# One hybrid decoder block on one core: the x, q and k projections of groups 1 to 7 take 512-column matmuls, one output half after the other

## The chip, the core and the metric

The kernel runs on one core of a Trainium2 chip. A core has a matrix engine (TensorE, PE in the profile, with its weight loads as PEld), a vector engine (VectorE, DVE), a scalar engine (ScalarE, ACT), GpSimd (POOL) and SyncE (SP), which issues most of the DMAs. Each engine works through its own list of instructions in the order in which the program was built and waits on semaphores for the others. The metric is device time in microseconds (us) for one execution; less is better.

## What is computed

The reference is one layer of a hybrid block on 256 tokens of 1024 channels, all in float32:

```python
hn = rmsnorm(x, norm1_w)
proj = hn @ w_in
z, xbc_raw, dt_raw, q, k, v, g_raw = jnp.split(proj, IN_OFFSETS, axis=-1)
...
y_ssd = ssd_mixer(z, xbc_raw, dt_raw, ...)       # x, B, C through a causal conv of 4 taps and SiLU, then the scan
q = partial_rope(q.reshape(b, s, ATT_N_HEADS, ATT_HEAD_DIM), pos)
k = partial_rope(k.reshape(b, s, ATT_N_HEADS, ATT_HEAD_DIM), pos)
y_att = moba_attention(q, k, v.reshape(b, s, ATT_N_HEADS, ATT_HEAD_DIM))
gates = jax.nn.sigmoid((g_raw + b_gate).astype(jnp.float32)).astype(x.dtype)
merged = g_ssd * (y_ssd @ w_ssd_proj) + g_att * (y_att @ w_att_proj)
x = x + merged @ w_out
h2 = rmsnorm(x, norm2_w)
a, gb = jnp.split(h2 @ w_ffn_up, 2, axis=-1)
a = causal_dwconv(a, ffn_conv_w, ffn_conv_b)
x = x + (jax.nn.silu(a) * gb) @ w_ffn_down
```

A final rmsnorm follows. The change is in `hn @ w_in`, in the columns that become x (the scan's input), q and k.

## The kernel before

**Products in two parts.** A float32 product is made of products of rounded parts. Each weight tile `raw` (128 partitions, 8 k-tiles of 256 columns, 1 MB) is split into a high part `hi` (an ACT copy that rounds, L95) and a rest `lo = raw - hi` (DVE, L103), each in two halves of 4 k-tiles. The activations `hn` are pairs in the same way: `hn[k][:, 0]` high, `hn[k][:, 1]` low, 256 tokens each, side by side. `mm_unit` (L145) makes, for each k-tile and each of two output halves m of 128 columns, three matmuls of 256 columns into the same sums: high weight by high (L164), high by low (L165), low weight by high (L166). That is 48 matmuls in a unit.

**Units and groups.** The weights come in units of 1 MB. Each of the 8 groups g has six units: bc (B and C), x, qk, then z and two of the gates for even g, or v and z for odd g (group 1 has no v; in group 7 z stands ahead of v). `next_unit` splits one unit ahead. `hi` and `lo` have 4 buffers of half a unit each, so a half of unit n+2 can be split when the same half of unit n has been read for the last time. The order of TensorE is the order in which the code is written; the order on ACT and DVE is made by a scheduler when the program is built, by priority and its own estimates of time.

**What stands between the units.** PSUM tiles `mm` have 3 buffers, taken in turn: one for each unit, two for a pair of gate units. After the unit bc, `conv_silu` (L382) reads its sums out of PSUM: an ACT pass makes `cacc`, three DVE steps (L391) add the other taps, for each of two halves, then `th` (ACT, L394) and the product (DVE, L395). x goes the same way. The unit qk is copied out by ACT to `qkraw` (L433), from which POOL's DMAs take the swapped rows for the rotation and DVE makes `qk` (L439). `small_1(g)` stands between the units x and qk on TensorE: the scan's products `py` of the group before (L519), the scores `s_ps` (L548), the attention output `po` (L585) and the broadcast `pb` (L241). On DVE and ACT the same step brings `yg` (L523, L524, L535), the softmax (L555 to L563), and the pairs `yatt` and `yn` (L203, L204).

Further on, the up projection's `mm_wide` (L168) makes the high weight's two products in one matmul of 512 columns (L174), then the low weight's in one of 256 (L178); its two sums meet when they are read out (L865, L866).

Of the kernel before, what the change touches and what calls it, by code (L numbers as in the profile page):

```python
# [8 lines left out]
F32 = mybir.dt.float32  # L9
F32R = mybir.dt.float32r  # L10
I32 = mybir.dt.int32
AF = mybir.ActivationFunctionType
ALU = mybir.AluOpType
PSUM = bass.MemoryType.PSUM
DRAM = bass.MemoryType.DRAM
PE_ONLY = {mybir.EngineType.PE}
IN_ORDER = {mybir.EngineType.PE, mybir.EngineType.Activation, mybir.EngineType.DVE}

P = 128
T = 256  # L20
# [21 lines left out]
def block_kernel(tc, xtok_d, head_d, par_d, nf_d, con_d, rope_d, win_d, wgate_d, bg_d, watt_d, wssd_d, wout_d, wup_d, wdn_d, out_d):  # L42
    nc = tc.nc
    st = ExitStack()
    pool = lambda name, bufs=1, **kw: st.enter_context(tc.tile_pool(name=name, bufs=bufs, **kw))
    with st:
# [36 lines left out]
        def new_pair(name):  # L83
            return pairs.tile([P, 2, T], F32R, tag="pair", bufs=32, name=name)
# [8 lines left out]
        def split_high(raw, k0, n):  # L93
            hi = wpool.tile([P, 4, 256], F32R, tag="hi", bufs=4, name="hi")
            split_half.hi = nc.scalar.activation(hi[:, :n], raw[:, k0 : k0 + n], AF.Copy)  # L95
            return hi
# [36 lines left out]
        def next_unit():  # L133

            i = next_unit.i
            next_unit.i += 1
            load_to(i + 3)
            while len(units) < min(i + 2, len(seq)):
                n = len(units)
                units.append(split_unit(raws[n], seq[n][1]))  # L140
            return units[i]
# [3 lines left out]
        def mm_unit(ps, halves, act, first=True, last=True, k0=0, apart=False):  # L145


            tiles = [(hi, lo, kk) for hi, lo, n in halves for kk in range(n)]
            nk = len(tiles)
            km = [(k, m) for k in range(nk) for m in range(2)]  # L150
            if apart:
                km.sort(key=lambda x: x[1])
                ps = [p[:, 0, :] for p in ps]
            else:
                ps = [ps[:, m, :] for m in range(2)]
            with tc.manual_schedule(engines=PE_ONLY):
                for k, m in km:
                    hi, lo, kk = tiles[k]
                    xh, xl = act[k0 + k][:, 0, :], act[k0 + k][:, 1, :]
                    wh = hi[:, kk, m * P : m * P + P]  # L160
                    wl = lo[:, kk, m * P : m * P + P]
                    a = first and k == 0 and (m == 0 or apart)
                    z = last and k == nk - 1 and (m == 1 or apart)
                    nc.tensor.matmul(ps[m], wh, xh, start=a, stop=False)  # L164
                    nc.tensor.matmul(ps[m], wh, xl, start=False, stop=False)  # L165
                    nc.tensor.matmul(ps[m], wl, xh, start=False, stop=z)  # L166
# [31 lines left out]

        def mm_tile():
            return ps_mm.tile([P, 2, T], F32, tag="mm", bufs=3, name="mm")  # L200

        def split_pair(dst, src):
            nc.scalar.activation(dst[:, 0, :], src, AF.Copy)  # L203
            nc.vector.tensor_tensor(dst[:, 1, :], src, dst[:, 0, :].bitcast(F32), op=ALU.subtract)  # L204
# [70 lines left out]
        flat = lambda ap: ap.rearrange("p a b -> p (a b)")  # L275
# [5 lines left out]
        hn = [new_pair("hn") for _ in range(KD)]  # L281
# [3 lines left out]
        with tc.manual_schedule(engines=IN_ORDER):  # L285
# [64 lines left out]
            for k in range(4):  # L350
                normed(k)
                for m in range(2):
                    nc.tensor.matmul(psbc[:, m], raws[0][:, k, m * P : m * P + P], hnf[k], start=(k == 0 and m == 0),
                                     stop=False)
# [3 lines left out]
            hi = split_high(raws[0], 4, 4)  # L358
# [38 lines left out]
        S = [dict() for _ in range(NG)]  # L397
# [11 lines left out]

        def u_x(g):  # L410
            hv = next_unit()
            ps = mm_tile()
            mm_unit(ps, hv, hn)
            xs = S[g]["xs"] = ssp.tile([P, 2, T], F32, tag="xs", bufs=2, name="xs")
            if g:
                conv_silu(xs, ps, (2 * g, 2 * g + 1))
            else:
                S[g]["x_ps"] = ps
# [5 lines left out]
        def u_qk(g):  # L424
            hv = next_unit()
            if g == 0:

                with tc.issue_after(split_half.lo.ins):
                    conv_silu(S[0]["xs"], S[0]["x_ps"], (0, 1))
            ps = mm_tile()  # L430
            mm_unit(ps, hv, hn)
            raw = atp.tile([P, 2, T], F32, tag="qkraw", bufs=1, name="qkraw")
            S[g]["qk_copy"] = nc.scalar.activation(raw, ps, AF.Copy)  # L433
            sw = swaps[g % 2]
            nc.gpsimd.dma_start(sw[48:80:2], raw[49:80:2])
            nc.gpsimd.dma_start(sw[49:80:2], raw[48:80:2])
            qk = S[g]["qk"] = atp.tile([P, 2, T], F32, tag="qk", bufs=2, name="qk")
            cosb = rope[:, 0:1, :].to_broadcast([P, 2, T])
            nc.vector.tensor_tensor(qk, raw, cosb, op=ALU.mult)  # L439
# [206 lines left out]
        atp = st_at.enter_context(tc.tile_pool(name="atp", bufs=1))  # L646
# [143 lines left out]
        for h in range(2):  # L790
            ps = [mm_tile(), mm_tile()]
# [4 lines left out]
            for c in range(2):  # L796
                m = half(mt[:, c], h)
# [33 lines left out]
        hv = next_unit()  # L831
# [7 lines left out]
        act = []  # L839
        first = []  # L840
        for f in range(2):
            hv, ps = next_unit(), mm_tile()
# [7 lines left out]
        for f in range(NF):  # L850
            ab = work.tile([P, 2, T], F32, tag="ab", bufs=2, name="ab")
            if f < 2:
                hv, ps = first[f]
# [5 lines left out]
            else:  # L859
# [3 lines left out]
                hv, ps = next_unit(), up.tile([P, 2, 2, T], F32, tag="up", bufs=2, name="up")  # L863
# [60 lines left out]
        for h in range(2):  # L924
            ps = [mm_tile(), mm_tile()]
            for k0, _ in DOWN[:-1]:
                mm_tok(ps, next_unit(), act, k0, NF)
            hv, k0 = next_unit(), DOWN[-1][0]
# [129 lines left out]
```

## Time and profile before

| | |
|---|---|
| median of 3 runs | 597.99 us (595.78 to 967.97) |
| profiled execution | 595.27 us, its span 593.5 us, so 1.77 us lie around the span |
| granted clock of TensorE | 0.998 |
| busy | PE 584.9 us (99%), DVE 458.8 us (77%), ACT 375.6 us (63%) |
| groups 1 to 7 | x units from about 60 us to 282 us into the span |

Matmuls overlap in their pipeline, so the time that a matmul takes from the engine is the distance from its start to the next one's start, not the duration shown beside it. The same holds on DVE and ACT to a lesser degree.

### The profile page before, as it was taken

What the parts mean: (1) busy time and instruction counts of PE and PEld (TensorE: products, weight loads), DVE (VectorE), ACT (ScalarE), POOL (GpSimd) and SP (SyncE); (2) the same over time, 40 slices, a digit from 0 to 9 for tenths busy, and PEclk for the clock granted to TensorE, in tenths of its full rate; (3) what the DMA queues carried; (4) which work ended last, traced back from release to release, by engine and by line L of the source; (5) the groups of instructions that cost most, each with busy time, mean ns of one, the idle gap of its engine ahead of it and who ended that gap; (6) DMA issues with size and microseconds to landing.
All of it is one profiled execution on the core that took longest, in us unless ns stands there. A gap on an engine that the chain in (4) does not pass through costs nothing.

```text
span 593.5 us, 9945 instructions
## 1 busy us (share of the span) xinstructions
PE 584.9 (99%) x3832; PEld 525.8 (89%) x3832; DVE 458.8 (77%) x891; ACT 375.6 (63%) x673; POOL 21.2 (4%) x41
## 2 busy tenths in 40 slices
PE   9999999999999999999999999999999999999994
PEld 8998999999999999999988888889888888888884
DVE  3896989888897888978896546667888898884643
ACT  2855696957769577695786333456877777774432
POOL 0010010100001000010000000000000000000100
PEclk9999999999999999999999999999999999999999
DMA  8666626662646526565345765545456456464611
GB/s 307 259 193 242 236 105 233 207 213 89 217 174 206 202 97 213 180 192 204 109 145 168 293 195 172 200 163 193 151 204 214 170 184 214 139 219 149 233 43 71
DMA packets 17936, 109.74 MB, mean 185 GB/s; under 512 B 2256, under 2 KB 2512, under 8 KB 6240
## 3 DMA queue, kind: packets, MB, share of 16 engines
q1 hardware_dynamic: 15120, 100.42, 48.2%
q0 software_dynamic: 2336, 6.85, 4.2%
q10 hardware_dynamic: 432, 1.84, 0.8%
q8 instruction: 30, 0.49, 0.3%
q14 instruction: 18, 0.15, 0.1%
HBM read 107.49 MB, written 1.08 MB: 183 GB/s over the span
## 4 chain that ended last, share of the span: by engine, by line
PE 99%; DVE 0%; issue 0%; ACT 0%; DVEq 0%; ACTq 0%
PE up L174 12%; PE mm L164 11%; PE mm L165 11%; PE mm L166 11%; PE mm L195 11%; PE mm L196 11%; PE mm L197 11%; PE up L178 6%; PE py L519 2%; PE mm L293 1%; PE s_ps L548 1%; PE po L585 1%; PE mm L458 1%; PE mm L459 1%; PE mm L460 1%; PE pt_ps L571 1%
## 5 line engine op out<-in xcount | busy, mean ns | idle before, releaser
L103 DVE TENSOR_TENSOR lo<-raw,hi 128x1024 fp32r<-128x1024 f32 x183 | 222.9, 1223 | 72.9 <-ACT hi L95 71.1
L95 ACT ACTIVATE hi<-raw 128x1024 fp32r<-128x1024 f32 x183 | 191.8, 1056 | 126.7 <-PE mm L197 64.1
L164 PE MATMUL mm<-hn,hi 128*128 128x256 f32 x504 | 143.6, 285 | 0.0
L165 PE MATMUL mm<-hn,hi 128*128 128x256 f32 x504 | 142.6, 283 | 0.0
L166 PE MATMUL mm<-hn,lo 128*128 128x256 f32 x504 | 142.5, 283 | 0.0
L164 PEld LDWEIGHTS mm<-hn,hi 128*128 128x128 f32 x504 | 96.7, 192 | 0.5 <-ACT hi L95 0.3
L165 PEld LDWEIGHTS mm<-hn,hi 128*128 128x128 f32 x504 | 96.7, 192 | 0.2
L166 PEld LDWEIGHTS mm<-hn,lo 128*128 128x128 f32 x504 | 96.7, 192 | 0.0
L174 PE MATMUL up<-xw,hi 128*128 128x512 f32 x320 | 76.3, 391 | 0.0
L174 PEld LDWEIGHTS up<-xw,hi 128*128 128x128 f32 x320 | 58.8, 188 | 11.4
L391 DVE SCALAR_TENSOR_TENSOR cacc<-mm,par,cacc 128x255 f32<-128x255 f32 (+2 forms) x96 | 44.4, 475 | 0.7
L178 PEld LDWEIGHTS up<-xw,lo 128*128 128x128 f32 x320 | 41.0, 191 | 1.6
L178 PE MATMUL up<-xw,lo 128*128 128x256 f32 x320 | 41.5, 283 | 0.0
L196 PE MATMUL mm<-lo,act 128*128 128x512 f32 (+1 forms) x92 | 35.0, 380 | 0.0
L195 PE MATMUL mm<-hi,act 128*128 128x512 f32 (+1 forms) x92 | 34.9, 380 | 0.0
L197 PE MATMUL mm<-hi,act 128*128 128x512 f32 (+1 forms) x92 | 34.9, 380 | 0.0
L875 DVE SCALAR_TENSOR_TENSOR facc<-ab,par,facc 128x255 f32<-128x255 f32 (+1 forms) x44 | 21.2, 483 | 11.4 <-ACT facc L873 10.6
L195 PE MATMUL mm<-hi,hn 128*128 128x512 f32 x64 | 25.4, 397 | 0.0
L195 PE MATMUL mm<-hi,yn 128*128 128x512 f32 x64 | 25.2, 394 | 0.0
L197 PE MATMUL mm<-hi,hn 128*128 128x512 f32 x64 | 25.0, 390 | 0.0
L196 PE MATMUL mm<-lo,hn 128*128 128x512 f32 x64 | 25.0, 390 | 0.0
L197 PE MATMUL mm<-hi,yn 128*128 128x512 f32 x64 | 24.9, 390 | 0.0
(208 smaller groups left out, 970.8 us busy)
## 6 DMA issues: line engine op xcount, KB each, us to landing
raw<-in_win_dram SPq DMA_DIRECT2D x34, 1024.0 KB, 4.8
raw<-in_wup_dram SPq DMA_DIRECT2D x22, 1024.0 KB, 4.8
raw<-in_wdn_dram SPq DMA_DIRECT2D x10, 1024.0 KB, 4.8
raw<-in_wgate_dram SPq DMA_DIRECT2D x8, 1024.0 KB, 5.3
raw<-in_wssd_dram SPq DMA_DIRECT2D x8, 1024.0 KB, 4.9
acsB<-acsT_d POOLq DMA_DIRECT2D x8, 512.0 KB, 5.8
raw<-in_watt_dram SPq DMA_DIRECT2D x4, 1024.0 KB, 5.3
raw<-in_wout_dram SPq DMA_DIRECT2D x4, 1024.0 KB, 5.2
```

Of the source, the lines that this page charges most:

```text
L95: split_half.hi = nc.scalar.activation(hi[:, :n], raw[:, k0 : k0 + n], AF.Copy)
L103: split_half.lo = nc.vector.tensor_tensor(lo[:, :n], raw[:, k0 : k0 + n], hi[:, :n].bitcast(F32), op=ALU.subtract)
L164: nc.tensor.matmul(ps[m], wh, xh, start=a, stop=False)
L165: nc.tensor.matmul(ps[m], wh, xl, start=False, stop=False)
L166: nc.tensor.matmul(ps[m], wl, xh, start=False, stop=z)
L174: nc.tensor.matmul(ps[:, m].rearrange("p a b -> p (a b)"), hi[:, kk, m * P : m * P + P], act[k].rearrange("p a b -> p (a b)"), start=(k == ...
L178: nc.tensor.matmul(ps[:, m, 1], lo[:, kk, m * P : m * P + P], act[k][:, 0, :], start=False, stop=(k == len(tiles) - 1))
L195: nc.tensor.matmul(o, xh, wh, start=(k == 0 if apart else k0 + k == 0), stop=False)
L196: nc.tensor.matmul(o, xh, wl, start=False, stop=False)
L197: nc.tensor.matmul(o, xl, wh, start=False, stop=(k0 + k == nk - 1))
L391: nc.vector.scalar_tensor_tensor(acc[:, s:], src[:, m, : T - s], w(m, 3 - s), acc[:, s:], op0=ALU.mult, op1=ALU.add)
L875: nc.vector.scalar_tensor_tensor(acc[:, s:], src[:, : T - s], w(2 - s), acc[:, s:], op0=ALU.mult, op1=ALU.add)
```

## The change

For g of 1 to 7, `u_x` and `u_qk` call `mm_sum` in place of `mm_unit`. It makes output half m = 0 in full, then m = 1, each in a PSUM tile of its own: 8 matmuls of 512 columns (high weight, both parts of hn), then 8 of 256 columns (low weight, high part of hn) that add to the second part of the tile. Each half is read out on its own: ACT copies the second part to SBUF, DVE adds the first part. For x the sum lands in a new tile `xsum`, from which `conv_silu` now reads; it has the tag and the single buffer of `qkraw`. Group 0, bc, z, v and the gates stay as they are.

```diff
+        def mm_sum(dst, halves, act):
+
+
+            tiles = [(hi, lo, kk) for hi, lo, n in halves for kk in range(n)]
+            for m in range(2):
+                ps = mm_tile()
+                with tc.manual_schedule(engines=PE_ONLY):
+                    for k, (hi, lo, kk) in enumerate(tiles):
+                        nc.tensor.matmul(flat(ps), hi[:, kk, m * P : m * P + P], flat(act[k]), start=(k == 0), stop=False)
+                    for k, (hi, lo, kk) in enumerate(tiles):
+                        nc.tensor.matmul(ps[:, 1], lo[:, kk, m * P : m * P + P], act[k][:, 0, :], start=False,
+                                         stop=(k == len(tiles) - 1))
+                mm_sum.copy = nc.scalar.activation(dst[:, m], ps[:, 1], AF.Copy)
+                nc.vector.tensor_tensor(dst[:, m], ps[:, 0], dst[:, m], op=ALU.add)
...
         def u_x(g):
             hv = next_unit()
-            ps = mm_tile()
-            mm_unit(ps, hv, hn)
+            if g:
+                ps = atp.tile([P, 2, T], F32, tag="qkraw", bufs=1, name="xsum")
+                mm_sum(ps, hv, hn)
+            else:
+                ps = mm_tile()
+                mm_unit(ps, hv, hn)
...
-            ps = mm_tile()
-            mm_unit(ps, hv, hn)
-            raw = atp.tile([P, 2, T], F32, tag="qkraw", bufs=1, name="qkraw")
-            S[g]["qk_copy"] = nc.scalar.activation(raw, ps, AF.Copy)
+            if g:
+                raw = atp.tile([P, 2, T], F32, tag="qkraw", bufs=1, name="qkraw")
+                mm_sum(raw, hv, hn)
+                S[g]["qk_copy"] = mm_sum.copy
+            else:
+                ps = mm_tile()
+                mm_unit(ps, hv, hn)
+                raw = atp.tile([P, 2, T], F32, tag="qkraw", bufs=1, name="qkraw")
+                nc.scalar.activation(raw, ps, AF.Copy)
```

The scheduler makes another order of it. In the changed kernel a line's number is larger by 15 (from L214 on) or 24 (behind `u_qk`); the sum on DVE is L215 and the copy on ACT is L214.

DVE, group 1, before, from the first step of bc's conv on. `mm_674` is the PSUM tile of bc, `raw_758` the weight of z1, the unit behind qk1:

```order
L391 SCALAR_TENSOR_TENSOR cacc_727<-mm_674,par_75,cacc_727 128x255
L391 SCALAR_TENSOR_TENSOR cacc_727<-mm_674,par_75,cacc_727 128x254
L391 SCALAR_TENSOR_TENSOR cacc_727<-mm_674,par_75,cacc_727 128x253
L391 SCALAR_TENSOR_TENSOR cacc_728<-mm_674,par_75,cacc_728 128x255
L103 TENSOR_TENSOR lo_887<-raw_758,hi_885 128x1024
L395 SCALAR_TENSOR_TENSOR bc_726<-th_734,cacc_727 128x256
L391 SCALAR_TENSOR_TENSOR cacc_728<-mm_674,par_75,cacc_728 128x254
L391 SCALAR_TENSOR_TENSOR cacc_728<-mm_674,par_75,cacc_728 128x253
L103 TENSOR_TENSOR lo_891<-raw_758,hi_889 128x1024
L395 SCALAR_TENSOR_TENSOR bc_726<-th_740,cacc_728 128x256
```

The same place in the changed kernel:

```order
L406 SCALAR_TENSOR_TENSOR cacc_727<-mm_674,par_75,cacc_727 128x255
L406 SCALAR_TENSOR_TENSOR cacc_727<-mm_674,par_75,cacc_727 128x254
L215 TENSOR_TENSOR xsum_768<-mm_769,xsum_768 128x256
L406 SCALAR_TENSOR_TENSOR cacc_727<-mm_674,par_75,cacc_727 128x253
L406 SCALAR_TENSOR_TENSOR cacc_728<-mm_674,par_75,cacc_728 128x255
L406 SCALAR_TENSOR_TENSOR cacc_814<-xsum_768,par_75,cacc_814 128x255
L410 SCALAR_TENSOR_TENSOR bc_726<-th_734,cacc_727 128x256
L406 SCALAR_TENSOR_TENSOR cacc_728<-mm_674,par_75,cacc_728 128x254
L406 SCALAR_TENSOR_TENSOR cacc_814<-xsum_768,par_75,cacc_814 128x254
L406 SCALAR_TENSOR_TENSOR cacc_728<-mm_674,par_75,cacc_728 128x253
L406 SCALAR_TENSOR_TENSOR cacc_814<-xsum_768,par_75,cacc_814 128x253
L215 TENSOR_TENSOR xsum_768<-mm_791,xsum_768 128x256
```

The two splits of z1 have left this place, and x's sums and conv steps stand among bc's.

DVE, group 1, before, some 20 instructions further on, at the end of the softmax's first passes; `raw_883` is the weight of bc of group 2:

```order
L555 ISA pr_871,sm_872<-s_ps_856,con_76 128x256
L555 ISA sm_872 128x1
L103 TENSOR_TENSOR lo_955<-raw_883,hi_953 128x1024
L557 TENSOR_SCALAR sm_872<-sm_872 128x2
L103 TENSOR_TENSOR lo_959<-raw_883,hi_957 128x1024
```

The same place in the changed kernel, where `raw_758` is z1's weight as above and `raw_876` bc's of group 2:

```order
L579 ISA pr_864,sm_865<-s_ps_849,con_76 128x256
L579 ISA sm_865 128x1
L103 TENSOR_TENSOR lo_880<-raw_758,hi_878 128x1024
L581 TENSOR_SCALAR sm_865<-sm_865 128x2
L103 TENSOR_TENSOR lo_884<-raw_758,hi_882 128x1024
L585 RECIPROCAL sm_855<-sm_855 128x2
L215 TENSOR_TENSOR qkraw_886<-mm_887,qkraw_886 128x256
L103 TENSOR_TENSOR lo_939<-raw_876,hi_937 128x1024
```

The splits of z1 stand here now, and those of bc behind them. In groups 3, 5 and 7 it is the same: both splits of the unit behind qk (v, v and z) move from between bc's conv steps to behind the second L535. In groups 2, 4 and 6 the first split of z stays among the conv steps and the second moves to behind the second L535.

ACT, group 1, before, from bc's conv on:

```order
L387 ACTIVATE cacc_727<-mm_674,par_75 128x256
L387 ACTIVATE cacc_728<-mm_674,par_75 128x256
L95 ACTIVATE hi_885<-raw_758 128x1024
L394 ACTIVATE th_734<-cacc_727 128x256
L95 ACTIVATE hi_889<-raw_758 128x1024
L387 ACTIVATE cacc_821<-mm_768,par_75 128x256
```

And in the changed kernel:

```order
L402 ACTIVATE cacc_727<-mm_674,par_75 128x256
L402 ACTIVATE cacc_728<-mm_674,par_75 128x256
L214 ACTIVATE xsum_768<-mm_769 128x256
L402 ACTIVATE cacc_814<-xsum_768,par_75 128x256
L409 ACTIVATE th_734<-cacc_727 128x256
L95 ACTIVATE hi_878<-raw_758 128x1024
L95 ACTIVATE hi_882<-raw_758 128x1024
L214 ACTIVATE xsum_768<-mm_791 128x256
```

Both high copies of z1 stand ahead of the copy of x's second half, and behind the first conv pass of x's first half, which waits for the sum on DVE.

## Rows read from the trace of the kernel before

**Rows 1.** The page: span, busy time by engine, and the chain's shares by engine.

```profile
span 593.5 us, 9945 instructions
PE 584.9 (99%) x3832; PEld 525.8 (89%) x3832; DVE 458.8 (77%) x891; ACT 375.6 (63%) x673; POOL 21.2 (4%) x41
...
PE 99%; DVE 0%; issue 0%; ACT 0%; DVEq 0%; ACTq 0%
```

**Rows 2.** Windows from small_1(2) to (3) to (4): PE, PEld, DVE, ACT, POOL busy, clock, DMA.

```profile
93.50:133.40 39.90, 39.90 (x297) 36.67 (x298) 34.97 (x74) 27.83 (x57) 2.61 (x5) 1.00 0.62 206
133.40:168.00 34.60, 34.60 (x296) 33.31 (x296) 30.23 (x67) 24.88 (x53) 1.54 (x3) 1.00 0.49 166
```

**Rows 3.** Waits of the weight loads: the one for a split, in total.

```profile
PEld mm L164 <- ACT hi L95: 0.3, 1, 0.3
```

**Rows 4.** Timeline of PE inside an `mm_unit`: start, duration, instruction.

```profile
149.79 0.28 PE L166 MATMUL mm<-hn,lo 128*128 128x256 f32 x1
...
150.15 0.28 PE L166 MATMUL mm<-hn,lo 128*128 128x256 f32 x1
```

**Rows 5.** The chain in the up projection: start, length, what.

```profile
414.61 3.65 PE up L174 x16
418.27 1.91 PE up L178 x16
420.18 3.65 PE up L174 x16
```

**Rows 6.** Groups of instructions by line and shape: busy us, mean ns, idle before.

```profile
L391 DVE SCALAR_TENSOR_TENSOR cacc<-mm,par,cacc 128x255 f32<-128x255 f32 x32 | 15.2, 476 | 0.0
...
L875 DVE SCALAR_TENSOR_TENSOR facc<-ab,par,facc 128x255 f32<-128x255 f32 x22 | 10.6, 483 | 10.6 <-ACT facc L873 10.6
...
L857 DVE TENSOR_TENSOR ab<-mm,rb 128x256 f32<-128x256 f32 x2 | 0.8, 417 | 0.0
...
L203 ACT ACTIVATE yatt<-po 128x256 fp32r<-128x256 f32 x8 | 3.0, 381 | 6.4 <-PE po L585 6.4
```

**Rows 7.** Timeline of DVE in group 1 (no idle between these rows).

```profile
65.10 1.90 DVE L391 SCALAR_TENSOR_TENSOR cacc<-mm,par,cacc 128x255 f32<-128x255 f32 x4
66.92 1.22 DVE L103 TENSOR_TENSOR lo<-raw,hi 128x1024 fp32r<-128x1024 f32 x1
68.05 0.42 DVE L395 SCALAR_TENSOR_TENSOR bc<-th,cacc 128x256 f32<-128x256 f32 x1
68.39 0.99 DVE L391 SCALAR_TENSOR_TENSOR cacc<-mm,par,cacc 128x254 f32<-128x254 f32 x2
...
76.67 1.22 DVE L103 TENSOR_TENSOR lo<-raw,hi 128x1024 fp32r<-128x1024 f32 x1
```

**Rows 8.** Timeline of PE in group 1: end of small_1, start of qk1.

```profile
67.22 0.93 PE L548 MATMUL s_ps<-qk 64*128 64x128 f32 x8
68.08 0.39 PE L164 MATMUL mm<-hn,hi 128*128 128x256 f32 x1
```

**Rows 9.** Timeline of DVE in group 3.

```profile
129.83 1.91 DVE L391 SCALAR_TENSOR_TENSOR cacc<-mm,par,cacc 128x255 f32<-128x255 f32 x4
...
134.38 1.22 DVE L103 TENSOR_TENSOR lo<-raw,hi 128x1024 fp32r<-128x1024 f32 x1 [0.28 <-ACT hi L95]
...
143.33 1.22 DVE L103 TENSOR_TENSOR lo<-raw,hi 128x1024 fp32r<-128x1024 f32 x1
```

**Rows 10.** Timeline of PE in group 3: start of x3, start of qk3.

```profile
127.45 0.28 PE L164 MATMUL mm<-hn,hi 128*128 128x256 f32 x1
...
136.88 0.36 PE L164 MATMUL mm<-hn,hi 128*128 128x256 f32 x1
```

**Rows 11.** Timeline of DVE in group 4.

```profile
169.06 1.23 DVE L103 TENSOR_TENSOR lo<-raw,hi 128x1024 fp32r<-128x1024 f32 x1 [0.34 <-ACT hi L95]
...
178.00 1.22 DVE L103 TENSOR_TENSOR lo<-raw,hi 128x1024 fp32r<-128x1024 f32 x1
```

**Rows 12.** Timeline of PE in group 4: start of qk4.

```profile
171.55 0.36 PE L164 MATMUL mm<-hn,hi 128*128 128x256 f32 x1
```

## The prediction, made before the result was known

> **What bounds the kernel now.** I read the page's busy shares and the chain that ended last first. TensorE is busy 584.9 us of a span of 593.5, and the chain is TensorE for 99% [rows 1]. A busy TensorE could still be waiting inside, so the waits come next: in all the groups the only wait of a weight load for a split is 0.3 us [rows 3]. From group 1 to 7 TensorE runs without a gap: what its instructions need is always there. So whatever shortens its list shortens the run, and whatever makes it wait once lengthens it, since no later idle time takes a wait back. The windows say how near the others are: from small_1(2) to small_1(3), 39.9 us, DVE is busy 34.97 and ACT 27.83; in the next 34.6 us, 30.23 and 24.88 [rows 2]. DVE has some 4.4 to 4.9 us to spare in a group. That is enough on average, so the question is the order within a group: what TensorE waits for next if DVE's list shifts.
>
> **TensorE's part.** Inside a unit of `mm_unit` the same line returns every 0.36 us, three matmuls [rows 4], so a unit of 48 takes 16 x 0.36 = 5.76 us. The up projection already runs the new form: 16 matmuls of 512 columns take 3.65 us and 16 of 256 take 1.91, and the next tile follows at once, 5.57 us after the first [rows 5]. The new order (8 wide, 8 narrow, twice) has the same counts. Each changed unit gains 0.19 us, the 14 of them 14 x 0.19 = 2.7 us. The bound below is zero gain, if a wide matmul took as long as two narrow ones (0.24 us); I take 2.7, since rows 5 are the same instructions at the same clock.
>
> [...] Rows 5 put a wide matmul at 3.65/16 = 0.228 us and a narrow one at 1.91/16 = 0.119, 0.010 us less for one wide than for two narrow. [...]
>
> **What comes on ACT and DVE.** For each x and each qk DVE gets two sums of 256 columns out of PSUM, 0.417 us each like L857 [rows 6]; in a row of busy work such an instruction takes 0.34 us of DVE's time (68.05 to 68.39 [rows 7]). Four in a group make 1.4 us, against 4.4 idle. ACT gets two copies for x and two in place of one for qk, 0.38 us each like the one of `yatt` [rows 6], under 1.2 us a group against 10 idle. Both fit, so as mere work I cost them at nothing. x's conv now reads SBUF. Its DVE steps: 476 ns out of PSUM (L391) and 483 ns out of SBUF in the FFN's like step (L875) [rows 6], so no change. PSUM tiles, three in turn: x and qk now take two each, so qk's first half needs the tile of bc, one unit earlier than that tile was needed before.
>
> **Where TensorE will wait: group 1.** Here DVE is late already. It begins bc's conv at 65.10 [rows 7], while small_1 follows x1 on TensorE and qk1 starts at 68.08 [rows 8]. First, qk1 needs bc's PSUM tile. Up to bc's last step DVE now has eight conv steps, one sum and one product (L410): at 0.455 us a step (65.10 to 66.92 for four) and 0.34 for the others that is at most 4.3 us, so the tile comes free at 69.0 to 69.4, and TensorE, 0.19 us earlier after x1, waits from 67.89: 1.1 to 1.5 us. Second, z1. Its first split now stands where the first split of bc2 stood, at 76.67 [rows 7]. Ahead of it two splits of 1.13 us (66.92 to 68.05) have gone and two sums of 0.34 have come: 76.67 - 2.26 + 0.68 = 75.1. The second sum may wait for its copy on ACT, behind the two high copies, so I add 0.2 (0 to 0.6): 75.3, done at 76.5. Without waits z1 would need it at its third matmul, 67.89 + 5.57 + 0.24 = 73.7. So group 1 loses 2.8 us in total, the 1.1 to 1.5 at qk1 among them; 2.0 to 3.4 with the bounds. Queued behind the late split on DVE are z1's other split, q and k's sums and bc2's splits; z1's second half is needed 2.9 us after its first, the split takes 1.2, and in group 2 TensorE itself is late, so nothing more is lost there.
>
> **Groups 3, 5, 7.** In group 3 the split of v3 stands where 143.33 stood [rows 9]. Gone: two splits (2.26) and the idle 0.28 ahead of one [rows 9]. Come: two sums (0.68). And the first sum waits for x3's first half: x3 starts at 127.45 [rows 10], its half is made after 5.57/2 = 2.8 us, the pipeline adds 0.2 and the copy 0.4, so 130.85 to 130.9; DVE gets there at 129.83 + 2 x 0.455 = 130.74 [rows 9]. That is a wait of 0.15. So 143.33 - 2.54 + 0.83 = 141.6, done at 142.85. TensorE: qk3 started at 136.88 [rows 10], v3 would start 5.76 later, less 0.38 saved by then, and needs the split at its second matmul, so at 142.4. Wait: 0.45 us, between 0 and 1.0. The same rows stand in groups 5 and 7, 74.5 and 149.1 us later; in group 7 z is behind qk and needs the split 0.12 later. Together 1.3 us (0 to 3). The tile of bc is no trouble here: bc's last step is done about 134.0, qk3 comes at 136.7.
>
> **Groups 2, 4, 6.** Only z's second split has moved, to where 178.00 stood in group 4 [rows 11]. One split and 0.34 of idle go [rows 11], 0.83 comes: 177.4, done 178.6. Needed at the middle of z4: 171.55 [rows 12] + 5.76 - 0.38 + 2.88 + 0.24 = 180.05. Nothing is lost, with 1.4 us to spare.
>
> **The sum.** 595.27 for the profiled execution (593.5 span and 1.77 around it) - 2.7 + 2.8 + 1.3 = 596.7 us. The three runs' median, 597.99, lies 2.7 above the profiled one, their lowest 0.5 above; I predict 597.0. Two per cent, 12 us, is about what a measurement of this kernel can tell from no change.
>
> **Rivals.** (a) No waits: the gain stands alone, 595.27 - 2.7 = 592.6. For it: the idle 4.4 us a group on DVE, and a trace in which almost no wait shows. Against it: group 1, where the tile of bc alone costs over 1 us. (b) More waits: the orders were laid out by estimates, and an engine that stands in order passes its lateness on. DVE waits for the copies on ACT, ACT for DVE's sum ahead of its high copies, and each us that DVE comes later to the split of v or z beyond the above is a us of TensorE in groups 1, 3, 5, 7, and in 2, 4, 6 from 1.4 us on. With 1.5 us more in each: 596.7 + 4 x 1.5 + 3 x 0.1 = 603, slower than before. It decides once DVE stands idle over 0.5 us ahead of `xsum`. Beyond 2% it would take 3.5 us in every group, which only an order that idles DVE for most of a half unit would give. (c) The wide matmul saves nothing: its 224 then cost what the narrow ones did, and 595.27 + 4.1 = 599.4. The rows say 0.228 against 0.24, so this is unlikely. [...] (d) The conv out of SBUF is quicker. Six steps a group stand ahead of the split that TensorE waits for; if each fell from 476 ns to the 417 of the quickest 256-column step in rows 6, that is 6 x 0.06 = 0.4 us off each of four waits, 596.7 - 1.6 = 595.1. The 483 ns out of SBUF [rows 6] speak against it. [...]
>
> **How the numbers follow.** Forecast 0.55; (a) 0.18; (b) 0.18; (c) 0.05; (d) 0.04. The range goes from (a)'s 592.6, less half a microsecond, to near (b)'s 603: 592 to 602. My forecast's own bounds, 595.27 - 2.7 + 2.0 to 595.27 - 2.7 + 6.4 and the 2.7 between profiled run and median, lie within it. All cases lie within 2%; I leave 0.03 for slower (an order that idles DVE in every group) and 0.01 for faster.
>
> **What would show it.** In the profile after: x and qk units of 5.57 us; L210's matmuls 0.228 us apart; in group 1 a wait of qk1 for `cacc` on DVE of 1.1 to 1.5 us and one of z1 for `lo` of about as much; in groups 3, 5, 7 waits for `lo` of 0.3 to 0.6; none in 2, 4, 6; the up projection and all behind it unchanged. I am wrong if those waits are absent (then a) or if every group waits over 1 us (then b), or if the chain leaves TensorE.

## The result, and the profile after the change

The changed kernel takes 600.36 us (median of 6 runs, 599.41 to 601.58); the kernel before takes 597.2 beside it (median of 6, 594.60 to 967.97). The ratio, 1.0066 with a 95% interval of [1.0042, 1.0089], leaves out the one execution of 967.97 us, which is no ordinary one: within 2%, but slower, by 3.9 us. The profiled execution took 599.41 us with a span of 597.6, against 595.27 and 593.5, so 4.1 us more. The forecast was 597.0 with a range of 592 to 602. The profiled execution is the quickest of the six: the other five took 600.01 to 601.58 us, at a mean granted clock of 0.991 to 0.994 against its 0.995. What the trace shows below is the mildest case, and where the others lost more is not shown.

The page of the changed kernel: span, busy time by engine, the granted clock in 40 slices, and the chain's shares by engine.

```profile
span 597.6 us, 9528 instructions
PE 584.0 (98%) x3608; PEld 514.5 (86%) x3608; DVE 467.5 (78%) x919; ACT 379.6 (64%) x694; POOL 21.3 (4%) x41
...
PEclk9999989999999999999999999999999999999998
...
PE 88%; DVE 4%; ACT 4%; DMA 3%; issue 1%; ACTq 0%; DVEq 0%
```

Two things differ from [rows 1]. The chain leaves TensorE for 11% of the span, most of it early: it runs over DMA, ACT and DVE. And the clock line has an 8 in its sixth slice, some 75 to 90 us. Group 1 lies there. TensorE's timeline from the first to the second `s_ps` of small_1 (units and waits only):

```profile
66.38 0.93 PE L572 MATMUL s_ps<-qk 64*128 64x128 f32 x8
...
67.94 2.11 PE L210 MATMUL mm<-hn,hi 128*128 128x512 f32 x8 [0.64 <-DVE xsum L215]
69.89 1.11 PE L212 MATMUL mm<-hn,lo 128*128 128x256 f32 x8
...
77.87 0.39 PE L166 MATMUL mm<-hn,lo 128*128 128x256 f32 x1 [3.83 <-DVE lo L103]
...
92.88 2.00 PE L210 MATMUL mm<-hn,hi 128*128 128x512 f32 x8
94.72 1.11 PE L212 MATMUL mm<-hn,lo 128*128 128x256 f32 x8
...
98.55 1.52 PE L543 MATMUL py<-mx,xt 128*64 128x256 f32 x16
```

Two waits stand where the forecast had them: qk1 waits 0.64 us, for `xsum` and not for `cacc`, and z1 waits 3.83 us for its low part. The next `s_ps` comes at 100.00, 33.62 us after this one; in the kernel before it came 27.67 us after it (67.22 [rows 8] to 94.89). Behind the wait the matmuls come slowly. The windows of 2 us there (busy PE, PEld, DVE, ACT, POOL, granted clock, DMA share, GB/s):

```profile
75.00:77.00 2.00, 0.00 (x0) 0.00 (x0) 1.95 (x10) 2.00 (x6) 0.00 (x0) 1.00 0.00 0
77.00:79.00 2.00, 1.13 (x9) 1.13 (x10) 2.00 (x4) 1.69 (x5) 0.00 (x0) 1.00 0.00 0
79.00:81.00 2.00, 2.00 (x12) 2.00 (x12) 2.00 (x6) 1.56 (x5) 0.00 (x0) 0.53 0.34 106
81.00:83.00 2.00, 2.00 (x13) 2.00 (x13) 1.18 (x3) 1.20 (x2) 0.35 (x1) 0.62 1.11 401
83.00:85.00 2.00, 2.00 (x19) 2.00 (x19) 1.72 (x2) 0.55 (x2) 0.64 (x2) 1.00 0.87 340
```

After the idle time the granted clock is down from about 79 to 82.4 us (0.52 over that stretch); 12 or 13 matmuls fit into 2 us there, where 19 fit at 1.00. From the starts: one every 0.215 us between 79.05 and 82.42, every 0.12 us before and behind. That loses (82.42 - 79.05) x (1 - 0.12 / 0.215) = 1.5 us.

What set the end of z1's wait is DVE, which came late into the group. Its timeline:

```profile
62.61 1.76 DVE L521 TENSOR_TENSOR mx<-mx,cb 128x1536 f32<-128x1536 f32 x1 [1.35 <-ACT mx L519]
64.29 2.35 DVE L103 TENSOR_TENSOR lo<-raw,hi 128x1024 fp32r<-128x1024 f32 x2
66.56 0.99 DVE L406 SCALAR_TENSOR_TENSOR cacc<-mm,par,cacc 128x255 f32<-128x255 f32 x2
67.47 0.42 DVE L215 TENSOR_TENSOR xsum<-mm,xsum 128x256 f32<-128x256 f32 x1
...
70.09 0.48 DVE L406 SCALAR_TENSOR_TENSOR cacc<-mm,par,cacc 128x253 f32<-128x253 f32 x1
...
71.03 0.43 DVE L215 TENSOR_TENSOR xsum<-mm,xsum 128x256 f32<-128x256 f32 x1
...
76.59 1.22 DVE L103 TENSOR_TENSOR lo<-raw,hi 128x1024 fp32r<-128x1024 f32 x1
```

The conv of bc1 begins at 66.56, where it began at 65.10 [rows 7]. Everything ahead of it hangs on `mx`, and `mx` on a DMA: `acsB`, the decays of group 0, which go through memory. ACT's first `mx`, of the kernel before and then of the changed one:

```profile
54.56 0.70 ACT L492 ACTIVATE mx<-acsB,acs 128x128 f32<-128x128 f32 x2 [2.91 <-DMA acsB<-acsT_d]
```

```profile
56.02 0.69 ACT L516 ACTIVATE mx<-acsB,acs 128x128 f32<-128x128 f32 x2 [5.35 <-DMA acsB<-acsT_d]
```

GpSimd issued that read at 48.42 us in both executions. It landed after 6.1 us in one and after 7.6 in the other, and the 1.46 us come out again, to the hundredth, at the conv. In all sixteen profiles of this document the conv begins 10.54 or 10.55 us after ACT's first `mx`. The write of the decays ahead of the read differed as well: it was issued at 43.60 and took 4.5 us before, at 42.62 and 5.5 us in the changed kernel, so that a head start of 0.98 us was lost in it.

Beyond group 1 the change gains. The start of each small_1's `s_ps`, in us, of three kernels (the third is an experiment below):

| | 1 | 2 | 3 | 4 | 5 | 6 | 7 | 8 |
|---|---|---|---|---|---|---|---|---|
| before | 67.22 | 94.89 | 134.75 | 169.43 | 209.29 | 243.97 | 283.83 | 306.99 |
| changed | 66.38 | 100.00 | 139.53 | 174.19 | 213.72 | 248.39 | 287.93 | 311.13 |
| splits_early | 66.32 | 96.48 | 136.01 | 170.36 | 209.89 | 244.24 | 283.77 | 306.77 |

At the second one the changed kernel is 5.11 us behind the kernel before, at the last 4.14.

### The profile page after: what moved, and what is told of

It reads as the page before. It is cut to its first block, busy times and chain, and to the rows that moved or that the text cites. A ratio compares the mean times of both kernels' runs of the same rounds, so it can differ in the third digit from the quotient of the medians.

```text
span 597.6 us, 9528 instructions
## 1 busy us (share of the span) xinstructions
PE 584.0 (98%) x3608; PEld 514.5 (86%) x3608; DVE 467.5 (78%) x919; ACT 379.6 (64%) x694; POOL 21.3 (4%) x41
## 3 DMA queue, kind: packets, MB, share of 16 engines
q10 hardware_dynamic: 432, 1.84, 0.8%
## 4 chain that ended last, share of the span: by engine, by line
PE 88%; DVE 4%; ACT 4%; DMA 3%; issue 1%; ACTq 0%; DVEq 0%
PE up L174 12%; PE mm L195 10%; PE mm L196 10%; PE mm L197 10%; PE up L178 6%; PE mm L166 6%; PE mm L164 6%; PE mm L165 6%; PE mm L210 6%; PE mm L212 3%; DMA acsB<-acsT_d 1%; PE mm L308 1%; PE py L543 1%; ACT hi L95 1%; PE mm L483 1%; DVE lo L103 1%
## 5 line engine op out<-in xcount | busy, mean ns | idle before, releaser
L103 DVE TENSOR_TENSOR lo<-raw,hi 128x1024 fp32r<-128x1024 f32 x183 | 222.8, 1223 | 69.3 <-ACT hi L95 67.7
L166 PE MATMUL mm<-hn,lo 128*128 128x256 f32 x280 | 80.2, 286 | 3.8 <-DVE lo L103 3.8
L164 PE MATMUL mm<-hn,hi 128*128 128x256 f32 x280 | 80.3, 287 | 0.0
L165 PE MATMUL mm<-hn,hi 128*128 128x256 f32 x280 | 79.9, 285 | 0.0
L174 PEld LDWEIGHTS up<-xw,hi 128*128 128x128 f32 x320 | 58.8, 188 | 11.4
L166 PEld LDWEIGHTS mm<-hn,lo 128*128 128x128 f32 x280 | 54.4, 194 | 4.2 <-DVE lo L103 4.0
L210 PE MATMUL mm<-hn,hi 128*128 128x512 f32 x224 | 57.0, 396 | 0.7 <-DVE xsum L215 0.6
L164 PEld LDWEIGHTS mm<-hn,hi 128*128 128x128 f32 x280 | 54.5, 195 | 0.2
L165 PEld LDWEIGHTS mm<-hn,hi 128*128 128x128 f32 x280 | 54.5, 195 | 0.2
L210 PEld LDWEIGHTS mm<-hn,hi 128*128 128x128 f32 x224 | 40.1, 189 | 8.7 <-DVE xsum L215 1.0
L212 PEld LDWEIGHTS mm<-hn,lo 128*128 128x128 f32 x224 | 30.5, 190 | 2.2
L212 PE MATMUL mm<-hn,lo 128*128 128x256 f32 x224 | 31.2, 282 | 0.0
L195 PE MATMUL mm<-hi,hn 128*128 128x512 f32 x64 | 25.4, 397 | 0.0
L516 ACT ACTIVATE mx<-acsB,acs 128x128 f32<-128x128 f32 x64 | 22.0, 390 | 5.4 <-DMA acsB<-acsT_d 5.4
```

The costliest lines, as they stand in the source:

```text
L103: split_half.lo = nc.vector.tensor_tensor(lo[:, :n], raw[:, k0 : k0 + n], hi[:, :n].bitcast(F32), op=ALU.subtract)
L174: nc.tensor.matmul(ps[:, m].rearrange("p a b -> p (a b)"), hi[:, kk, m * P : m * P + P], act[k].rearrange("p a b -> p (a b)"), start=(k == ...
L195: nc.tensor.matmul(o, xh, wh, start=(k == 0 if apart else k0 + k == 0), stop=False)
L210: nc.tensor.matmul(flat(ps), hi[:, kk, m * P : m * P + P], flat(act[k]), start=(k == 0), stop=False)
L212: nc.tensor.matmul(ps[:, 1], lo[:, kk, m * P : m * P + P], act[k][:, 0, :], start=False, stop=(k == len(tiles) - 1))
```

## The experiments

Ratios are to the kernel before, on the same chip, with their 95% intervals. In the first four, theory A puts the loss into group 1 (z1's split behind the convolution of x1 on DVE, and the clock behind the wait); B puts it into the new form wherever it stands; C, in splits_ahead, says that DVE is late in group 1 because the decays land late, whatever its order.

**from_group_2.** Group 1 as before, groups 2 to 7 changed.

```diff
-            if g:
+            if g >= 2:
```

(in `u_x` and in `u_qk`)

> mm_sum only in groups 2 to 7; group 1 keeps mm_unit. Theory A (the loss sits in group 1: z1's first split comes late on DVE, TensorE waits and its clock falls): 12 units gain 0.19 us each, 2.3 us, the short waits in groups 3, 5 and 7 keep about 1.1, so 1.2 us less than before, ratio 0.998, and no wait of TensorE over 1 us in group 1. Rival B (the added work on DVE and ACT, or the wide matmuls themselves, cost in every group): six sevenths of the 3.9 us stay, ratio 1.005 to 1.006.

Measured: 596.34 us, ratio 1.0000 [0.998, 1.0021]. The loss is gone, so it is group 1's; but no gain shows either. The profile has two reasons. `acsB` landed late in it (ACT waited 5.47 us), and group 1, whose code is that of the kernel before, took 29.23 us instead of 27.67. TensorE waits there in another place:

```profile
82.27 1.53 PE L595 MATMUL pt_ps<-con,pr 128*128 128x128 f32 x6 [0.94 <-ACT pr L587]
```

So a late landing seems to cost the code of the kernel before some 1.5 us as well; of the 1.56, the wait shown is 0.94. And group 2 lost 0.63 us to z2's split.

**only_group_1.** The other half: `if g == 1:` in both places.

> mm_sum only in group 1, all other groups as before. Theory A: 0.4 us gained by two units, about 6 us lost by the waits and the clock of group 1, so 5 to 6 us more than before, ratio 1.008 to 1.010. Rival B: one seventh of the loss, ratio 1.000 to 1.001.

Measured: 598.35 us, 1.0058 [1.0032, 1.0084]. A, though with less than A's size. `acsB` landed early in its profile (ACT waited 2.74 us): z1 waits 2.25 us, the clock falls to 0.50 in the window from 78 to 80, and group 1 takes 31.50 us.

**splits_ahead.** The whole change, and in group 1 the conv of x1 is held behind the next unit's splits, as group 0 does it.

```diff
-            if g:
+            if g > 1:
                 conv_silu(xs, ps, (2 * g, 2 * g + 1))
...
-            if g == 0:
+            if g < 2:
                 with tc.issue_after(split_half.lo.ins):
-                    conv_silu(S[0]["xs"], S[0]["x_ps"], (0, 1))
+                    conv_silu(S[g]["xs"], S[g]["x_ps"], (2 * g, 2 * g + 1))
```

> The whole change, but in group 1 the conv of x is released only behind the splits of the unit after qk (as group 0 does it already), so z1's splits stand ahead of it on DVE. Theory A: the wait of z1 and the fall of the clock go, 2.7 us gained less 1.1 in groups 3, 5, 7 and up to 0.7 at qk1, so 0.5 to 1.5 us less than before, ratio 0.997 to 0.999. Rival C (DVE is late in group 1 because the scan's decays land late, whatever its order): z1 still waits some 2 us or more, ratio 1.003 or higher.

Measured: 596.8 us, 1.0026 [1.0007, 1.0046]. Group 1 is cured: 27.34 us, 0.33 less than before the change. But group 2 takes 41.86, 2.0 more:

```profile
106.72 0.39 PE L166 MATMUL mm<-hn,lo 128*128 128x256 f32 x1 [2.07 <-DVE lo L103]
```

Now z2's second split is late, which neither theory had foreseen, and the ratio lies above A's 0.997 to 0.999. C's sign, a wait of z1, did not show; but `acsB` landed early in this profile (ACT waited 3.18 us), so the run says little of a late landing.

**filled_wait.** The whole change with 14 small products of `ones` by `ones` on TensorE between qk1 and z1, whose result nothing uses. They fill the wait with work.

```diff
             u_qk(g)
+            if g == 1:
+                fill = ps_s.tile([P, 2, T], F32, tag="ss", bufs=2, name="fill")
+                for _ in range(14):
+                    nc.tensor.matmul(fill[:, 0, 0:P], ones, ones, start=True, stop=True)
```

> The whole change, with 14 matmuls of ones (128 columns, float32, results unused) on TensorE between qk1 and z1, about 3.1 us of work in the wait for z1's split. Theory A with the clock as a part: z1's matmuls stay 0.12 us apart, and the time falls by about 1.5 us against the change, to ratio 1.004. If the fall of the clock costs nothing in the end (DVE sets the pace behind it too): as the change, 1.0066. If the wait is shorter in these runs than the filler, the filler adds its excess.

Measured: 597.8 us, 1.0045 [1.0025, 1.0066], granted clock 1.00 behind the filler: z1's matmuls start 0.12 us apart, from 76.12 to 79.00. The group takes 30.44 us. `acsB` landed early in its profile (ACT waited 3.01 us), as in only_group_1, which is the fair neighbour: 31.50 us there, with the clock at 0.50. With work in the wait the clock stayed, and useless work was worth 1.06 us (1.32, if the group is counted from DVE's conv, as in the table further down).

In the next four, A is a theory of a full DVE: between 61 and 112 us it has no free time, so what is put on it comes out as a wait.

**qk_only.** Only q and k in the new form (`u_x` as before).

> Only q and k of groups 1 to 7 are computed in the new form; x keeps its three matmuls of 256 columns. VectorE's order in group 1 is then that of the kernel before (both halves of z1's split ahead of the convolution of x1). Theory A (VectorE has no free time between about 61 and 112 us, and what is put on it there comes out as a wait of TensorE): 7 x 0.19 = 1.3 us are saved, 0.75 us of sums per group lie behind z's splits and cost little, ratio 0.998 to 1.001, and no wait of z1 for its split. Rival B (output halves in turn keep the banks too long, wherever the form is used): 1.003 and more, with waits at z or v.

Measured: 598.86 us, 1.0038 [1.0015, 1.006]. A missed. The splits are early, yet TensorE waits:

```profile
71.67 2.08 PE L210 MATMUL mm<-hn,hi 128*128 128x512 f32 x8 [0.91 <-DVE cacc L406]
77.59 0.36 PE L164 MATMUL mm<-hn,hi 128*128 128x256 f32 x1 [2.89 <-ACT hi L95]
```

The second wait is put down to ACT, but both splits of z1 had long been made. What ended then on DVE is the last conv step of x1 out of PSUM (76.97, 0.47 long). That fits three PSUM tiles in turn: with x in one tile and q and k in two, z1 gets the tile of x1. The half of the change makes a wait of its own. I had not foreseen it.

**x_only.** Only x in the new form (`u_qk` as before).

> Only x of groups 1 to 7 is computed in the new form; q and k are as before. VectorE's order in group 1 is that of the change: both halves of z1's split behind the convolution of x1. Theory A: TensorE waits 1.5 to 3.5 us in group 1 for z1's split, and the clock falls behind it; ratio 1.002 to 1.006. Rival B: half of the loss of the whole change, 1.002 to 1.003, without one long wait in group 1.

Measured: 600.96 us, 1.0077 [1.0051, 1.0104], more than either theory said. Its profile: z1 waits 3.67 us for its low part, the clock falls to 0.50. The new form of x alone moves z1's split back, and loses as much as the whole change.

**rope_on_gpsimd.** The whole change, RoPE of groups 1 to 7 on GpSimd.

```diff
-            nc.vector.tensor_tensor(qk, raw, cosb, op=ALU.mult)
+            (nc.gpsimd if g else nc.vector).tensor_tensor(qk, raw, cosb, op=ALU.mult)
```

(and the two products in `turn_qk` likewise)

> The whole change, and the three VectorE instructions of RoPE of groups 1 to 7 (0.68 us each) run on GpSimd. In VectorE's order z1's split stands ahead of RoPE, so group 1 is not helped. Theory A: the wait in group 1 stays (2 to 4 us, and what the clock loses behind it), the one in group 2 goes; ratio 1.003 to 1.006, periods of the later groups shorter by up to 0.3 us each. Rival C (GpSimd's instructions slow VectorE's or come too late for the attention scores): ratio 1.008 and more.

Measured: 600.75 us, 1.0061 [1.0034, 1.0088]. As A had it for group 1: z1 waits 3.35 us. But the later groups are no shorter than in the changed kernel (39.54 and 34.70 us from one `s_ps` to the next). The profile says why: DVE was not freed. 21 products of 0.68 us left it, 14.4 us in all, and yet it is busy 469.4 us against 467.5. Its other instructions took longer, the splits above all. The splits in the changed kernel, then in this run; below, an instruction of DVE on 128 x 2, which takes 0.16 us elsewhere, and the product on GpSimd beside it:

```profile
L103 DVE TENSOR_TENSOR lo<-raw,hi 128x1024 fp32r<-128x1024 f32 x183 | 222.8, 1223 | 69.3 <-ACT hi L95 67.7
```

```profile
L103 DVE TENSOR_TENSOR lo<-raw,hi 128x1024 fp32r<-128x1024 f32 x183 | 233.2, 1282 | 70.2 <-ACT hi L95 68.5
...
89.80 1.80 DVE L236 SCALAR_TENSOR_TENSOR ry<-ra,ry 128x2 f32<-128x2 f32 x1
90.27 1.30 POOL L472 TENSOR_TENSOR qk<-qk,swap 128x512 f32<-128x512 f32 x1
```

C's condition, GpSimd slowing DVE, holds then, though not its price of 1.008 and more.

**ahead_and_rope.** The edits of splits_ahead and rope_on_gpsimd together.

> The whole change, the convolution of x1 held behind the next splits as in the run splits_ahead, and RoPE of groups 1 to 7 on GpSimd, which frees VectorE of 2.05 us per group. Theory A (a full VectorE, not the order alone): the wait of 2.1 us that splits_ahead showed at z2 goes, and what is left of the saving shows: ratio 0.995 to 0.998. If the order alone mattered, as splits_ahead: 1.002 to 1.003. Rival C (GpSimd slows VectorE or is late): 1.004 and more.

Measured: 598.35 us, 1.0022 [0.9996, 1.0048]. z2 waits 2.03 us, as it did with RoPE on DVE, and the wait ends 13.1 us after the second `s_ps` in both (108.90 - 95.78 and 106.72 - 93.58). This does not decide between DVE's amount of work and its order. No step of RoPE stands in that stretch, DVE works there without a gap in both profiles, and over the span it is busy 469.6 us against 466.7 in splits_ahead: it was not freed.

That left order against amount. In the next four, "order theory A" is the place of the split alone, F the amount of work.

**late_split.** The kernel *before*, with z1's two low parts put behind the conv of x1, and nothing else.

```diff
+                if n == 9:
+                    his = [split_high(raws[n], k0, 4) for k0 in (0, 4)]
+                    with tc.issue_after(conv_silu.end.ins):
+                        units.append([split_half(raws[n], 4 * j, 4, h) for j, h in enumerate(his)])
+                else:
+                    units.append(split_unit(raws[n], seq[n][1]))
```

(`n == 9` is z1; `conv_silu.end` is the last product of the conv written last, here that of x1)

> The kernel before, with one thing of the change: both halves of z1's split stand behind the convolution of x1 in VectorE's order. No matmul and no eviction is changed, and VectorE does no more work. Order theory A: TensorE waits 1.4 us and more for z1's split (z1 starts at 73.9, its first split would begin near 74.3 and take 1.2), and the clock falls behind the wait; ratio 1.0025 to 1.006. Rival F (it is the 0.74 us of sums per unit that overfill VectorE, whatever its order): 0.999 to 1.001.

Measured: 601.17 us, 1.0091 [1.0062, 1.0119]. The order alone, without a changed matmul or a sum, costs at least as much as the whole change; the two intervals overlap. `acsB` landed late in its profile (ACT waited 6.15 us). Timeline of TensorE and the windows behind it:

```profile
79.92 0.58 PE L171 MATMUL mm<-hn,lo 128*128 128x256 f32 x1 [5.68 <-DVE lo L103]
```

```profile
78.00:80.00 2.00, 0.08 (x1) 0.09 (x1) 2.00 (x8) 1.58 (x5) 0.00 (x0) 0.84 0.00 0
80.00:82.00 2.00, 2.00 (x9) 2.00 (x10) 2.00 (x3) 2.00 (x8) 0.00 (x0) 0.50 0.00 0
```

**splits_early.** The whole change, with the split of the unit behind q and k ranked ahead of the convs, in every group from 1 to 7.

```diff
-                units.append(split_unit(raws[n], seq[n][1]))
+                if n - 1 in qk_units:
+                    with tc.high_priority():
+                        units.append(split_unit(raws[n], seq[n][1]))
+                else:
+                    units.append(split_unit(raws[n], seq[n][1]))
```

(`qk_units` holds the places of q and k in the list of units)

> The whole change, and the split of the tile that follows q and k (z in groups 1, 2, 4, 6, v in 3, 5, 7) is ranked ahead of the convolutions in VectorE's order, in every group, as it stood before the change. Nothing else is changed. Order theory A: no wait for a split in groups 1 to 7, the saving of 2.7 us shows but for bank waits of up to 1.5 us: ratio 0.996 to 0.999. Rival F (overfull VectorE): the waits move to the banks of x and qk, 1.001 to 1.005.

Measured: 593.67 us, 0.9974 [0.9955, 0.9993]. The change becomes a gain. No wait for a split is left. F's sign, waits for a PSUM tile, shows in group 1 alone, at qk1, and its price does not:

```profile
67.77 2.11 PE L215 MATMUL mm<-hn,hi 128*128 128x512 f32 x8 [0.52 <-DVE xsum L220]
...
72.48 2.11 PE L215 MATMUL mm<-hn,hi 128*128 128x512 f32 x8 [1.65 <-DVE cacc L411]
```

**early_and_rope.** The same with RoPE on GpSimd.

> As splits_early, and RoPE of groups 1 to 7 on GpSimd, which frees VectorE of 2.05 us per group. Order theory A: the same time as splits_early within 0.15%. Rival F: at least 1 us less than splits_early, ratio 0.996 to 0.999.

Measured: 594.98 us, 0.999 [0.9973, 1.0007]: no better than splits_early. (The ratio differs by 0.16%, a hair more than A had it, within the intervals.) It is no test of F, though: DVE is busy 473.0 us against 466.6 in splits_early, so it was not freed here either. What speaks against F are the two runs before: late_split adds no work and loses, splits_early keeps all of the added work and gains.

**decays_scalar_queue.** The whole change; the decays of group 0 are written and read by ACT's queue instead of GpSimd's.

```diff
-            nc.gpsimd.dma_start(acsB, acsT_d[4 * g : 4 * g + 4, :].partition_broadcast(P))
+            (nc.gpsimd if g else nc.scalar).dma_start(acsB, acsT_d[4 * g : 4 * g + 4, :].partition_broadcast(P))
...
-                nc.gpsimd.dma_start(acsT_d, acsT)
+                nc.scalar.dma_start(acsT_d, acsT)
```

> The whole change; the decays of group 0 are written to and read from memory by ScalarE's queue, no longer GpSimd's (acsT_d and acsB; VectorE's order changes at one place only, near 44 us). If a late landing of acsB is part of the loss and this queue lands it earlier (wait of ScalarE under 3 us, where the changed kernel showed 5.35): ratio 1.003 to 1.005. If it lands as late as before, or the loss does not hang on it: 1.006 to 1.009.

Measured: 595.2 us, 0.9997 [0.9979, 1.0014], less than the expectation allowed. The split stands as late in DVE's list as in the changed kernel, and the loss is nearly gone. ACT waits only 2.30 us, bc1's conv begins at 64.39, and the wait of z1 is short:

```profile
75.70 0.39 PE L166 MATMUL mm<-hn,lo 128*128 128x256 f32 x1 [1.75 <-DVE lo L103]
```

In the windows behind it the clock is 1.00: this wait cost no clock.

Open then was whether the queue helps the kernel by itself, so two more ran.

**before_decays.** The kernel before with that queue edit.

> The kernel before with the queue edit of decays_scalar_queue alone (decays of group 0 by ScalarE's queue). If that queue helps only by landing acsB earlier for a VectorE that TensorE waits for, the kernel before, in which TensorE waits for nothing there in most executions, gains little: ratio 0.998 to 1.0, with fewer runs near 597. If the queue edit helps whatever the change: 0.994 to 0.996, about what it took off the changed kernel (0.7%).

Measured: 594.93 us, 0.998 [0.9966, 0.9994]. Little, as the first case had it, but its 12 runs lie within 594.2 to 595.5, where the kernel before beside it went from 594.3 to 598.4.

**early_decays.** splits_early with the queue edit.

> splits_early with the queue edit: the split of z or v ahead of the convolutions and the decays of group 0 by ScalarE's queue. If both took away the same loss (TensorE waiting for VectorE in group 1): 0.9955 to 0.9975, up to 1.5 us under splits_early since its bank wait of 1.65 us in group 1 shrinks with an earlier VectorE. If they add in full: 0.990 to 0.992.

Measured: 592.99 us, 0.9947 [0.9928, 0.9966], between the two cases, nearer to "the same loss": splits_early's 0.26% and before_decays' 0.20% about add up. It beats the kernel before by about 3 us (0.53%). In its profile `acsB` still landed late (ACT waited 4.45 us; qk1's second half waits 1.65), so that the queue always lands it sooner is not shown.

Group 1 of eight of these kernels in one table (us): when DVE begins bc1's conv, when the next small_1's `s_ps` starts, the difference, z1's wait for its low part, the lowest clock of the 2 us windows behind it (0.53 and 0.55: these two windows begin at 79 and 78, the slow matmuls at 79.05 and 78.18).

| | conv | `s_ps` | difference | z1's wait | clock |
|---|---|---|---|---|---|
| changed | 66.56 | 100.00 | 33.44 | 3.83 | 0.53 |
| x_only | 66.66 | 100.09 | 33.43 | 3.67 | 0.50 |
| rope_on_gpsimd | 65.81 | 99.24 | 33.43 | 3.35 | 0.55 |
| only_group_1 | 64.11 | 97.72 | 33.61 | 2.25 | 0.50 |
| late_split | 67.82 | 101.98 | 34.16 | 5.68 | 0.50 |
| filled_wait | 64.49 | 96.78 | 32.29 | filled | 1.00 |
| decays_scalar_queue | 64.39 | 96.35 | 31.96 | 1.75 | 1.00 |
| before | 65.10 | 94.89 | 29.79 | none | 1.00 |

With the split late, the end of group 1 is the start of that conv plus 32.0 to 32.3 us, plus 1.1 to 1.6 where the clock falls (late_split, with z1 in the same matmuls but q and k in the old form and another order, 0.6 more). When TensorE itself arrives, with its first `s_ps` between 66.2 and 67.1, makes no difference that the table shows.

## Why the prediction was wrong

The mechanism was right in the main: a late split of z1 makes TensorE wait in group 1, and short waits follow in groups 3, 5 and 7. The term of group 1 was mis-sized, and it decided the sign.

- **The gain.** Forecast 0.19 us a unit. x2 of the changed kernel takes 98.55 - 92.88 = 5.67 us to the next instruction; x3 before took 133.30 - 127.45 [rows 10] = 5.85, so 0.18. Over nine units, from the third `s_ps` to the eighth, splits_early gains 172.24 - 170.76 = 1.48 us, 0.16 each. Eight wide matmuls take 94.72 - 92.88 = 1.84 us, 0.230 each, near the 0.228 of [rows 5].
- **DVE's extra work.** Costed at nothing. Behind group 1 that fits: splits_early does all of this work, waits for no split, and is quicker than the kernel before by 0.16 us a unit. In group 1 it is open: there splits_early still waits 0.52 and 1.65 us at qk1 for DVE. The runs with RoPE on GpSimd can't tell, since DVE was not freed in them.
- **qk1.** Forecast was a wait of 1.1 to 1.5 us for bc's PSUM tile; measured, 0.64 us, and for another tile. qk1 starts at 67.94, right behind the sum of x's first half (67.47 and 0.42 long), while DVE reads bc's tile until 70.57 (70.09 and 0.48 long). So the tiles do not go strictly in turn in the changed kernel: qk's first half got the tile of x's first half. It changed nothing in the sum, because z1's wait behind it covers it.
- **Groups 3, 5, 7.** Forecast 1.3 us, measured 171.60 - 170.76 = 0.84: the changed kernel against splits_early over the same stretch. In group 3 the wait stands at the weight load: v3's second matmul is 0.33 behind its first (147.34 and 147.67) where 0.12 is usual, its load waits 0.26 for `lo`, and its split begins at 146.40. Groups 2, 4, 6: no wait was forecast, none shows.
- **Group 1, the step that failed:** "So group 1 loses 2.8 us in total, the 1.1 to 1.5 at qk1 among them; 2.0 to 3.4 with the bounds." Measured: the second `s_ps` comes 5.11 us later than before, with 0.56 gained in x1, qk1 and x2, so the loss is 5.7 us. (TensorE came to group 1 0.84 us earlier than in the kernel before, 66.38 against 67.22 [rows 8]; the wait took that in, since DVE set its end.) Three parts explain it. (1) From the conv's start to the end of z1's split I reckoned 76.5 - 65.1 = 11.4 us; it took 77.81 - 66.56 = 11.25. This part held. (2) The conv's start, 65.10 [rows 7], I took for a property of the kernel. It hangs on a DMA whose landing differs between executions: 1.46 us later here, and with DVE on the path that is 1.46 us of the run. (3) I had no term for the clock. The wait of 3.83 us took it down to 0.52 for 3.4 us: 1.5. So 2.8 - 0.15 + 1.46 + 1.5 = 5.6, against the 5.7.
- **The sum and the number.** My sum said 1.4 us more than the profiled execution; the profiled ones differ by 4.1. Of the 2.7 between, group 1 makes 2.9; groups 3, 5 and 7 cost 0.5 less than forecast, and the units gained some 0.3 less. Then I put 597.0 between the sum and the shown median of 597.99, which stated a time one us under that median while the sum said slower. That median was a poor start: the third of those runs is the one of 967.97, so 597.99 is the higher of the other two, and of the five others known now it is the highest. The spread of those runs, 2.2 us between the lowest and the median, I treated as noise around the kernel. before_decays suggests that much of it goes with this one DMA: with the other queue 12 runs lie within 1.3 us. (decays_scalar_queue and early_decays, with the same queue, still spread over 2.6 and 2.2.) The spread was a sign that the row from which the term started was one draw of several.
- **Rivals.** (a) fell with the first wait. (b), "the orders were laid out by estimates, and an engine that stands in order passes its lateness on", came nearest: the lateness was passed on, in one group rather than in all, though DVE stood idle for less than 0.1 us ahead of `xsum` there, where (b) had named 0.5. (c) fell with the 0.18. (d) fell: a conv step of 255 columns takes 476 ns out of PSUM and 477 out of SBUF in the changed kernel. That the chain left TensorE, the last sign named, came true as well, but the forecast's own waits on DVE would have brought it. The two groups of instructions (busy, mean ns):

```profile
L406 DVE SCALAR_TENSOR_TENSOR cacc<-mm,par,cacc 128x255 f32<-128x255 f32 x18 | 8.6, 476 | 0.0
...
L406 DVE SCALAR_TENSOR_TENSOR cacc<-xsum,par,cacc 128x255 f32<-128x255 f32 x14 | 6.7, 477 | 0.0
```

What stays open: why `acsB` lands 6.1 us after its issue in one execution and 7.6 in another, and whether ACT's queue lands it sooner or only steadies it. I can't tell from the changed kernel's six times in how many of them it landed late.

## What to carry to other kernels

When a change moves the instruction that feeds the busiest engine back in another engine's list, the price lies in its position more than in that engine's load, and its position starts from whatever it waited for last: trace that back to its own start, and if a DMA stands there, price the term for the DMA's late landings as well. A first wait of some us on TensorE can cost a second time through the clock (here 3.83 us of wait, then 1.5). Work that is moved to another engine has not freed the first until that one's busy time says so (here 467.5 us became 469.4). And after such a change look at the order before giving it up: here ranking one split ahead of the convs turned 0.66% lost into 0.26% gained, with the same instructions.

## What the runs showed of the hardware

- The clock does not follow from the length of the wait alone. It fell to 0.50 to 0.55 behind waits of 2.03 us (ahead_and_rope, 0.50 from 110 to 112), 2.25 (only_group_1), 3.35 (rope_on_gpsimd) and more, and stayed at 1.00 behind 1.75 (decays_scalar_queue). Behind 2.07 (splits_ahead) no fall shows: the next matmuls start 0.11 and 0.12 us apart, the mean clock of that execution is 0.998, and group 2 is 2.33 us longer than in the changed kernel (41.86 against 39.53), of which the wait is 2.07.
- In group 1 of rope_on_gpsimd, GpSimd took 1.29 to 1.65 us for a product of 128 x 512 that takes DVE 0.68 to 0.69, and DVE's instructions beside it became longer: the mean split went from 1223 to 1282 ns, and 14.4 us of products moved off DVE left its busy time no lower in any of the three runs (469.4 us against 467.5, 469.6 against 466.7, 473.0 against 466.6).
- One transfer of 512 KB, issued at the same instant (48.42 us) in two executions (before and changed), landed 1.5 us apart, after 6.1 and 7.6 us. In the changed kernel, where TensorE waits for what hangs on it, that is 1.46 us of the run.
